# First stage of a hybrid decoder step: three engines in a written-out order, roots of row tiles in pairs, transposes woven into the first projections

## The chip, the cores and the metric

The kernel runs on one core of a Trainium2 chip. The metric is the device time of one execution in microseconds (us). Engines: PE (TensorE, matmuls; its weight loads are shown as PEld), DVE (VectorE), ACT (ScalarE), POOL (GpSimd), and SP, which issues the DMA loads and stores.

## The reference, cut to what matters

A gated-DeltaNet layer and an attention layer run over 1024 prompt rows and 8 sample rows of width 1024. The change lies in the first stage, which norms the rows and makes the first projections:

```python
def rmsnorm(x, g):
    xf = x.astype(jnp.float32)
    y = xf * lax.rsqrt(jnp.mean(xf * xf, axis=-1, keepdims=True) + EPS)
    return (y * g.astype(jnp.float32)).astype(x.dtype)

def gdn_layer(x, conv_buf, s0, norm_g, w_in, conv_w, a_log, dt_bias, o_norm, w_out):
    proj = rmsnorm(x, norm_g) @ w_in
    qkv, gate, a, beta_logit = jnp.split(proj, [...], axis=-1)
    qkv, new_buf = causal_conv_silu(qkv, conv_buf, conv_w)
    ...
```

## The kernel before

The 1032 rows lie in nine tiles `xt` of 128 rows (the ninth has 8). For each tile ACT squares the row and sums it (`junk`, `r`), DVE turns the sum into a reciprocal root (`rsqrt`: nine small operations on one column, each reading the one before), DVE scales the tile in place by root and gain (`xt`), PE transposes it in two halves of four 128x128 blocks into a PSUM buffer (`xps`, from a pool `gen` of two buffers), ACT copies each half out as its high part and DVE subtracts to get the low part (both into `xg`, which keeps every value as a sum of two). A half's buffer is free again when DVE's subtraction has read it.

Tiles 0 to 2 make group 0 of the columns (384), tiles 3 to 5 group 1 (384), tiles 6 to 8 group 2 (264). For each group PE then makes `psab` (16 matmuls with the small weight `wabp`, for the decay and beta logits) and two conv projections of head 0, key and query (24 matmuls each: high weight by high part, low weight by high part, high weight by low part). Each weight of 128 columns is loaded in two halves of 256 KB into `raw` (two buffers), copied by ACT (`whi`) and subtracted by DVE (`wlo`). Behind the projections come the gate projection of head 0 (weight `wz`), and, on a high priority, the chain from `abT` over `pst` and `ab` to `gf`, `psg` and `eG`: the decays. `cps` are the transposes of the conv taps and of the conv state, 24 small ones, into `cvT`. From the program's line 543 on (631 in the change) a planner written in the kernel has set the order by its own costs.

In the stage itself the tile framework's scheduler sets each engine's order from program order, priorities and its own estimates; the code says only what depends on what. SP issues the loads in the order of the string `LO` (digits are x tiles, `g` the gain, `k` and `q` the two weights), and eight DMAs may be under way at once; a ninth waits for an earlier one.

Of the kernel before, what the change touches and what calls it, by code (L numbers as in the profile page):

```python
# [57 lines left out]
def hybrid_step(  # L58
# [37 lines left out]
    def gps(name, dt=F32):  # L96
        return gen.tile([P, 512], dt, tag="gen", name=name)
# [8 lines left out]
    ident = cst.tile([P, P], F32, name="ident")  # L106
# [3 lines left out]
    ones = cst.tile([P, P], F32, name="ones")  # L110
# [75 lines left out]
    def load_w(col, src):  # L186
        hi = whl.tile([P, KT, P], F32R, tag="whi", name="whi")
        lo = whl.tile([P, KT, P], F32R, tag="wlo", name="wlo")
        load_split(hi, lo, src[:, col:col + P].rearrange("(k p) c -> p k c", p=P))
        return hi, lo  # L190

    def proj_group(hi, lo, xt_, gn, ps):
        i = 0
        for w_, part in ((hi, 0), (lo, 0), (hi, 1)):
            for k in range(KT):
                mm(ps[:, :gn], w_[:, k, :], xt_[:, part, k, :gn], i == 0, i == 3 * KT - 1)
                i += 1
                yield 0
# [33 lines left out]
    with tc.tile_pool(name="p2a", reuse_waits="tile", bufs=1) as p2a, \  # L232
# [39 lines left out]
        V.tensor_copy(wabp[:, :, 0:16], wab)
        V.tensor_tensor(out=wabp[:, :, 32:48], in0=wab, in1=wabp[:, :, 0:16].bitcast(F32), op=ALU.subtract)
        cvr = p2a.tile([28, 3072], F32, name="cvr")
        DMA.dma_start(out=cvr[0:24], in_=state_conv[0].rearrange("b i c -> (b i) c"))
        DMA.dma_start(out=cvr[24:28], in_=conv_w_a[0])
        sel = p2a.tile([64, 16], F32, name="sel")
        V.tensor_tensor(out=sel, in0=ident[:64, 0:16], in1=ident[:64, 32:48], op=ALU.add)
        abT = p2a.tile([64, T], F32, name="abT")

        def first_proj(gi):
# [5 lines left out]
            for j, w in enumerate(ws0):  # L287
                m = (1 - j) * H
                if gi == 0:
                    ues.append((0, m, 1 - j, conv_open(m)))  # L290
                ps = pj.tile([P, 512], F32, tag="pj", name="pj")
                for _ in proj_group(*w, xg[gi], gn, ps):
                    pass
                conv_evac(ues[j][3], m, gi, ps)

        for t in range(NT + 1):
            n = P if t < NT else NS
            g, off = divmod(t * P, 384)
            xt = xts[t]
            junk = p1.tile([P, D], BF16, tag="junk", name="junk", bufs=1)  # L300
            r = sm.tile([P, 1], F32, tag="r1", name="r1")
            S.activation(junk[:n], xt[:n], AF.Square, accum_out=r[:n])
            ri = sm.tile([P, 1], F32, tag="ss", name="ri")
            rsqrt(ri[:n], r[:n], 1, 1.0 / D, EPS, n, tag="b")
            V.scalar_tensor_tensor(out=xt[:n], in0=xt[:n], scalar=ri[:n], in1=gbc[:n], op0=ALU.mult, op1=ALU.mult)
            for hf in range(2):
                ps = gps("xps").rearrange("p (k t) -> p k t", k=4)
                for k in range(4):
                    PE.transpose(ps[:, k, :n], xt[:n, ts(4 * hf + k, P)], ident[:n, :n])
                hi = xg[g][:, 0, 4 * hf:4 * hf + 4, off:off + n]  # L310
                S.copy(hi, ps[:, :, :n])
                V.tensor_tensor(out=xg[g][:, 1, 4 * hf:4 * hf + 4, off:off + n], in0=ps[:, :, :n],
                                in1=hi.bitcast(F32), op=ALU.subtract)
            if t == CT:
                for q in range(2):
                    ps = gps("cps")
                    for j in range(12):
                        PE.transpose(ps[:, j * 28:j * 28 + 28], cvr[:, ts(12 * q + j, P)], ident[:28, :28])
                    S.copy(cvT[:, 12 * q:12 * q + 12, :].rearrange("p a b -> p (a b)"), ps[:, :12 * 28])
                V.tensor_scalar_mul(cvT[:, :, 24:28], cvT[:, :, 24:28], 0.5)  # L320
# [1546 lines left out]
```

## Time and profile before

| | |
|---|---|
| median of 3 runs | 1298.4 us (1294.66 to 1300.23) |
| profiled execution, its own time | 1299.52 us |
| its span, first to last instruction | 1297.8 us |
| mean granted TensorE clock | 0.985 |
| first `psab` matmul | 27.05 us |
| first matmul of the next stage (line 543) | 82.46 us |

The profile is that of one execution, with the start and the duration of each instruction. Consecutive instructions of one kind are merged in its timeline ("x8"). The duration of a merged row reaches from the start of the first to the end of the last. Matmuls are pipelined, so the end of one lies behind the start of the next.

### The profile page before, as it was taken

How to read it: one execution, taken by the hardware profiler on the slowest of the kernel's cores; microseconds unless marked ns; L12 is line 12 of the kernel's file. 1: busy time of each engine (PE TensorE's matmuls, PEld its weight loads, DVE VectorE, ACT ScalarE, POOL GpSimd, SP SyncE). 2: the span in 40 equal slices, each digit the busy share in tenths (PEclk: the TensorE clock that was granted, in tenths of full speed). 3: DMA queues.
4: the chain of work that ended last, by engine and by line, in shares of the span. 5: the costliest groups of instructions: out<-in, count | busy, mean ns of one | idle time of the engine just before them, and what ended most of it. 6: DMA issues, size and time to landing. Idle time of an engine off the chain costs nothing.

```text
span 1297.8 us, 24347 instructions
## 1 busy us (share of the span) xinstructions
PE 1223.9 (94%) x8887; PEld 1110.2 (86%) x8887; DVE 925.4 (71%) x2656; ACT 633.7 (49%) x1812; POOL 287.4 (22%) x404
## 2 busy tenths in 40 slices
PE   3999999999999999998999978999999999999998
PEld 3989898989999988888988756888889888888898
DVE  7468988878979897787976349587685677677221
ACT  5236555645455453545443127375574566666100
POOL 1036433424324353343301122111030020000000
PEclk9999999999999999998999979999999999999899
DMA  7021111110221322110256656111020021002322
GB/s 240 1 81 35 36 29 40 37 51 18 68 66 36 98 65 86 36 36 17 67 158 209 203 200 203 39 52 31 3 74 9 3 74 35 26 2 88 123 86 73
DMA packets 131988, 92.03 MB, mean 71 GB/s; under 512 B 33881, under 2 KB 123713, under 8 KB 131809
## 3 DMA queue, kind: packets, MB, share of 16 engines
q1 hardware_dynamic: 131868, 90.48, 23.6%
q8 instruction: 70, 1.15, 0.4%
q14 instruction: 50, 0.40, 0.1%
HBM read 69.28 MB, written 23.25 MB: 71 GB/s over the span
## 4 chain that ended last, share of the span: by engine, by line
PE 66%; DVE 20%; ACT 5%; DMA 4%; issue 3%; POOL 2%; SPq 1%; DVEq 0%; ACTq 0%; POOLq 0%
PE pj L543 24%; PE pj L100 15%; PE ivt L543 4%; DVE co L543 3%; PE chB L543 3%; PE sps L100 2%; PE chA L543 2%; PE op L100 2%; DMA out_dram<-hx 1%; PE ptp L1646 1%; DVE wqkv L82 1%; PE sp L543 1%; PE tq L1593 1%; DVE f L543 1%; PE psab L100 1%
## 5 line engine op out<-in xcount | busy, mean ns | idle before, releaser
L543 PE MATMUL pj<-xg,whi 128*128 128x384 f32 (+1 forms) x1392 | 289.3, 335 | 1.0 <-ACT whi L543 1.0
L543 PEld LDWEIGHTS pj<-xg,whi 128*128 128x128 f32 x1392 | 222.0, 190 | 2.7 <-ACT whi L543 1.2
L100 PE MATMUL pj<-wqkv,ng 128*128 128x384 f32 x768 | 154.2, 344 | 0.0
L543 PE MATMUL pj<-xg,wlo 128*128 128x384 f32 (+1 forms) x696 | 153.2, 337 | 0.0
L543 DVE SCALAR_TENSOR_TENSOR co<-ue,cvT,co 128x528 f32<-128x528 f32 x144 | 134.5, 940 | 16.1 <-ACT co L543 14.5
L100 PEld LDWEIGHTS pj<-wqkv,ng 128*128 128x128 f32 x768 | 132.3, 190 | 4.6 <-issue 4.2
L543 PEld LDWEIGHTS pj<-xg,wlo 128*128 128x128 f32 x696 | 112.9, 191 | 1.4 <-issue 0.7
L93 POOL TENSOR_TENSOR raw<-raw,gains 128x512 f32<-128x512 f32 x40 | 45.7, 1152 | 254.4 <-DMA raw<-in_w_in_b_dram 178.7
L100 PE MATMUL pj<-wob,oh 128*128 128x384 f32 (+1 forms) x576 | 97.9, 324 | 0.3 <-DVE hx L1828 0.3
L100 PEld LDWEIGHTS pj<-wob,oh 128*128 128x128 f32 x576 | 90.2, 190 | 1.1 <-DVE hx L1828 0.5
L543 PE MATMUL pj<-woa,ohl 128*128 128x512 f32 x288 | 76.1, 406 | 0.0
L543 PEld LDWEIGHTS pj<-woa,ohl 128*128 128x128 f32 x288 | 51.8, 188 | 11.5 <-issue 1.5
L1828 DVE TENSOR_TENSOR hx<-hx,pj 128x384 f32<-128x384 f32 (+3 forms) x27 | 13.7, 507 | 64.8 <-PE pj L100 35.8
L543 ACT COPY ue<-pj 128x384 f32<-128x384 f32 (+1 forms) x88 | 31.7, 377 | 52.8 <-PE pj L543 45.8
L543 POOL TENSOR_TENSOR ue<-ue,co 128x528 f32<-128x528 f32 x24 | 33.9, 1412 | 72.4 <-ACT ue L543 72.4
L543 DVE TENSOR_TENSOR wlo<-raw,whi 128x512 fp32r<-128x512 f32 x58 | 43.6, 757 | 7.6 <-ACT whi L543 7.4
L543 ACT ACTIVATE ue<-co 128x528 f32<-128x528 f32 x48 | 30.8, 644 | 30.2 <-DVE co L543 27.9
L543 ACT CAST whi<-raw 128x512 fp32r<-128x512 f32 x58 | 35.8, 619 | 16.9 <-PE pj L543 16.5
L100 PE MATMUL pj<-woa,ohl 128*128 128x512 f32 x96 | 28.7, 453 | 11.2 <-DVE ohl L1421 5.7
L543 POOL TENSOR_TENSOR co<-co,ue 128x528 f32<-128x528 f32 x24 | 39.0, 1623 | 1.3
L100 PE MATMUL sps<-kTh,qst 128*128 128x256 f32 (+1 forms) x144 | 37.5, 297 | 0.9 <-DVE m L1623 0.9
L100 PE MATMUL sps<-kTl,qst 128*128 128x256 f32 (+1 forms) x144 | 35.9, 297 | 0.5 <-DVE kTl L1600 0.5
(906 smaller groups left out, 2935.2 us busy)
## 6 DMA issues: line engine op xcount, KB each, us to landing
raw<-in_w_in_a_dram SPq DMA_DIRECT2D x64, 256.0 KB
ssm<-in_state_ssm_dram SPq DMA_DIRECT2D x32, 256.0 KB
hD<-hx SPq DMA_DIRECT2D x16, 512.0 KB
raw<-in_w_in_b_dram SPq DMA_DIRECT2D x32, 256.0 KB
xt<-in_x_prompt_dram SPq DMA_DIRECT2D x8, 512.0 KB
out_dram<-ssm SPq DMA_DIRECT2D x16, 256.0 KB
raw<-in_w_out_a_dram SPq DMA_DIRECT2D x16, 256.0 KB
hx<-in_x_prompt_dram SPq DMA_DIRECT2D x8, 512.0 KB
```

Source lines behind the costliest of these rows:

```text
L82: V.tensor_tensor(out=lo, in0=raw, in1=hi.bitcast(F32), op=ALU.subtract)
L93: G.tensor_tensor(out=raw, in0=raw, in1=gain[:, k:k + n].unsqueeze(2).broadcast_to([P, n, c]), op=ALU.mult)
L100: PE.matmul(out, lhsT, rhs, start=start, stop=stop, skip_group_check=True)
L543: op.f(*op.a, **op.k)
L1593: PE.transpose(tq[:, ts(h, P)], qhl[:, h].rearrange("p a d -> p (a d)"), identr)
L1646: PE.transpose(pp[:, ts(h, P)], pr[h // 2][:, h % 2, ts(kt, P)], ident)
L1828: V.tensor_tensor(out=hx[:n, :cn], in0=hx[:n, :cn], in1=ps[:n, :cn], op=ALU.add)
```

## The change

The order of PE, DVE and ACT in the stage is now that of the code (`manual_schedule`), in a sequence written by hand. Only tiles 0 to 2 are transposed ahead of the first `psab`. The other tiles' transposes stand between the first conv matmuls, half a tile after every four (`weave`). The roots are taken for tile 0, then in pairs (1 and 2, 3 and 4, 5 and 6, 7 and 8): the nine operations work on two columns. Squares of the next pair stand ahead of the copies of the pair before. The first weight (key) has a raw tile of its own, `wk_raw`, loaded by one DMA; the second (query) is loaded and split inside the weave. Loads go in the order `0g12a34k5678q`: `wab` ahead of tile 3, the key weight behind tile 4, the query weight last. The conv taps are turned in group 1's first conv projection and the copies of the conv state into `ue` (`conv_open`) come after the stage's projections.

```diff
-LO = "0g12k345q678"
-CT = 5
+LO = "0g12a34k5678q"
...
+        wk_raw = p1.tile([P, KT, P], F32, name="wk_raw")
+        wk = [whl.tile([P, KT, P], F32R, tag=f"w{a}", name=f"w{a}") for a in ("hi", "lo")]
+        ws0 = [wk]
...
+            elif o == "k":
+                DMA.dma_start(out=wk_raw, in_=w_in_a[0][:, H * P:H * P + P].rearrange("(k p) c -> p k c", p=P))
...
+        def turn(t):
...
+                S.copy(hi, ps[:, :, :n])
+                V.tensor_tensor(out=xg[g][:, 1, 4 * hf:4 * hf + 4, off:off + n], in0=ps[:, :, :n],
+                                in1=hi.bitcast(F32), op=ALU.subtract)
+                yield
...
+        def root(tiles):
+
+            n_ = len(tiles)
+            r, ri = (sm.tile([P, 2], F32, tag=g_, name="r1") for g_ in ("r1", "ss"))
+            for i, t in enumerate(tiles):
+                rts[t] = (r[:, i:i + 1], ri[:, i:i + 1])
+
+            def chain():
+                rsqrt(ri[:, :n_], r[:, :n_], n_, 1.0 / D, EPS, tag="b")
...
+        def weave(a_, b_, n):
+
+            for i, _ in enumerate(a_):
+                if i % n == n - 1:
+                    next(b_, None)
+            for _ in b_:
+                pass
...
+        with tc.manual_schedule(engines={mybir.EngineType.PE, mybir.EngineType.DVE, mybir.EngineType.Activation}):
+            chain = root([0])
+            sums(0)
+            chain()
+            scales(0)
+            chain = root([1, 2])
+            sums(1, 2)
+            for _ in turns([0]):
+                pass
+            chain()
+            scales(1, 2)
+            V.tensor_copy(wabp[:, :, 0:16], wab)
+            V.tensor_tensor(out=wabp[:, :, 32:48], in0=wab, in1=wabp[:, :, 0:16].bitcast(F32), op=ALU.subtract)
+            chain34 = root([3, 4])
+            sums(3, 4)
+            for _ in turns([1, 2]):
+                pass
+            chain34()
+            scales(3)
+            for a in range(2):
+                split(wk[0][:, ts(a, 4)], wk[1][:, ts(a, 4)], wk_raw[:, ts(a, 4)])
+            scales(4)
+            chain56 = root([5, 6])
+            sums(5)
+            first_ab(0)
+            sums(6)
+            chain78 = root([7, 8])
+            weave(first_conv(0, 0), seq(turns([3]), do(chain56), do(scales, 5), turns([4]), do(scales, 6), do(second_w), do(sums, 7, 8), turns([5])), 4)
...
+            weave(first_conv(0, 1), seq(turns([6]), do(chain78), do(scales, 7), do(scales, 8), turns([7, 8])), 4)
+            first_ab(1)
+            weave(first_conv(1, 0), turn_taps(), 10)
...
+        for j in range(2):
+            conv_open(ues[j][3], ues[j][1])
```

DVE before, where the roots of tiles 5, 6 and 7 lie around the scale and the subtractions of tile 5 (`xt_184`; `rs_x`, `rs_u` and `ri` are the small tiles of a root, with one line of `rsq_x` for each operation, L122 to L134):

```order
L132 TENSOR_TENSOR rs_u<-rs_u,ri 128x1
L128 SCALAR_TENSOR_TENSOR rs_u<-rs_x,ri 128x1
L122 TENSOR_SCALAR rs_x<-r_454 128x1
L133 SCALAR_TENSOR_TENSOR rs_u<-rs_u 128x1
L129 TENSOR_TENSOR rs_u<-rs_u,ri 128x1
L126 TENSOR_SCALAR ri<-rs_x 128x1
L134 SCALAR_TENSOR_TENSOR ri<-rs_u,ri 128x1
L130 SCALAR_TENSOR_TENSOR ri<-rs_u,ri 128x1
L128 SCALAR_TENSOR_TENSOR rs_u<-rs_x,ri 128x1
L305 SCALAR_TENSOR_TENSOR xt_184<-xt_184,ri,gbc 128x1024
L312 TENSOR_TENSOR xg_98<-xps,xg_98 128x4x128 x2
```

Operations of three tiles' roots take turns. In the change, on DVE from the subtractions of tile 6 (`xg_99`) on, the root of tiles 7 and 8 (`r_322`, `r_323`) and the scale of tile 7 (`xt_188`):

```order
L296 TENSOR_TENSOR xg_99<-xps,xg_99 128x4x128 x2
L121 TENSOR_SCALAR rs_x<-r_322 128x2
L125 TENSOR_SCALAR r_323<-rs_x 128x2
L127 SCALAR_TENSOR_TENSOR rs_u<-rs_x,r_323 128x2
L128 TENSOR_TENSOR rs_u<-rs_u,r_323 128x2
L129 SCALAR_TENSOR_TENSOR r_323<-rs_u,r_323 128x2
L130 TENSOR_TENSOR rs_u<-rs_x,r_323 128x2
L131 TENSOR_TENSOR rs_u<-rs_u,r_323 128x2
L132 SCALAR_TENSOR_TENSOR rs_u<-rs_u 128x2
L133 SCALAR_TENSOR_TENSOR r_323<-rs_u,r_323 128x2
L285 SCALAR_TENSOR_TENSOR xt_188<-xt_188,r_323,gbc 128x1024
```

One root stands by itself, behind the subtractions of tile 6 and ahead of the scale of tile 7. PE in the same place, before (`xt_184` is tile 5, `xt_196` tile 6, `xt_198` tile 7; `pj` are the conv matmuls of group 0):

```order
L100 MATMUL pj<-xg_97,whi 128x384 x9
L318 MATMUL cps<-ident,cvr 128x28 x24
L100 MATMUL pj<-xg_97,whi 128x384
L309 MATMUL xps<-ident,xt_196 128x128 x8
L100 MATMUL pj<-xg_97,whi 128x384 x6
L100 MATMUL pj<-xg_97,wlo 128x384 x6
L309 MATMUL xps<-ident,xt_198 128x128 x4
```

and in the change (`xt_184` tile 5, `xt_186` tile 6, `xt_188` tile 7):

```order
L293 MATMUL xps<-ident,xt_184 128x128 x4
L99 MATMUL pj<-xg_97,whi 128x384 x4
L293 MATMUL xps<-ident,xt_186 128x128 x4
L99 MATMUL pj<-xg_97,whi 128x384 x4
L293 MATMUL xps<-ident,xt_186 128x128 x4
L99 MATMUL pj<-xg_97,wlo 128x384 x4
L293 MATMUL xps<-ident,xt_188 128x128 x4
L99 MATMUL pj<-xg_97,wlo 128x384 x4
```

Every half tile has four conv matmuls behind it, and `cps` is gone from here. PE at the start of the gate projection (`pj` from `xg_97` on), before:

```order
L100 MATMUL pj<-xg_99,whi 128x264 x8
L100 MATMUL pj<-xg_97,whi 128x384 x8
L100 MATMUL pj<-xg_97,wlo 128x384 x2
L100 MATMUL psg<-gf,mle 128x64
L100 MATMUL psg<-gf,mgt 128x64
L100 MATMUL psg<-gf,ones 128x64
L100 MATMUL pss<-esd,ones 128x128
L100 MATMUL pj<-xg_97,wlo 128x384 x6
```

and in the change:

```order
L99 MATMUL pj<-xg_99,whi 128x264 x8
L99 MATMUL psg<-gf,mle 128x64
L99 MATMUL psg<-gf,mgt 128x64
L99 MATMUL psg<-gf,ones 128x64
L99 MATMUL pss<-esd,ones 128x128
L99 MATMUL pj<-xg_97,whi 128x384 x8
L99 MATMUL pj<-xg_97,wlo 128x384 x8
```

`psg` and `pss` have moved from inside the gate projection to ahead of it; on ACT the copies of the gate's weight have moved from ahead of `eG` to behind it, and on DVE its two subtractions from inside the chain from `ab` to `gf` to behind it.

## Rows read from the trace of the kernel before

**Rows 1.** The page: span, busy time of PE, and the chain that ended last, by engine.

```profile
span 1297.8 us, 24347 instructions
...
PE 1223.9 (94%) x8887; PEld 1110.2 (86%) x8887; DVE 925.4 (71%) x2656; ACT 633.7 (49%) x1812; POOL 287.4 (22%) x404
...
PE 66%; DVE 20%; ACT 5%; DMA 4%; issue 3%; POOL 2%; SPq 1%; DVEq 0%; ACTq 0%; POOLq 0%
```

**Rows 2.** Windows: us, busy time of each engine, granted PE clock, DMA share, GB/s.

```profile
0.00:27.00 27.00, 7.43 (x32) 6.29 (x33) 19.19 (x83) 16.84 (x31) 4.44 (x19) 1.00 0.85 262
27.00:83.00 56.00, 54.90 (x359) 52.45 (x358) 26.53 (x93) 16.79 (x38) 0.77 (x4) 1.00 0.12 42
553.00:556.40 3.40, 3.40 (x17) 3.40 (x16) 2.63 (x4) 0.87 (x2) 3.00 (x3) 0.50 0.03 5
```

**Rows 3.** Timeline of PE: start, us, what, x count [idle before].

```profile
11.29 1.94 PE L309 MATMUL xps<-ident,xt 128*128 128x128 f32 x8 [11.29 <-DVE xt L305]
17.03 1.97 PE L309 MATMUL xps<-ident,xt 128*128 128x128 f32 x8 [3.79 <-DVE xg L312]
21.23 1.97 PE L309 MATMUL xps<-ident,xt 128*128 128x128 f32 x8 [2.24 <-DVE xg L312]
...
27.05 4.03 PE L100 MATMUL psab<-xg,wabp 128*128 128x384 f32 x12
...
34.09 0.60 PE L309 MATMUL xps<-ident,xt 128*128 128x128 f32 x4
...
37.88 1.67 PE L318 MATMUL cps<-ident,cvr 28*128 28x28 f32 x24
...
46.55 0.84 PE L100 MATMUL pst<-sel,abT 64*128 64x16 f32 x6
47.32 3.08 PE L100 MATMUL psab<-xg,wabp 128*128 128x384 f32 x16
...
70.38 0.41 PE L100 MATMUL psg<-gf,mle 128*128 128x64 f32 x2
...
82.46 1.68 PE L543 MATMUL pj<-xg,whi 128*128 128x384 f32 x8 [0.99 <-ACT whi L543]
```

**Rows 4.** Timeline of DVE, first stage.

```profile
8.12 0.15 DVE L122 TENSOR_SCALAR rs_x<-r 128x1 f32<-128x1 f32 x1 [2.63 <-ACT junk L302]
...
9.86 1.28 DVE L305 SCALAR_TENSOR_TENSOR xt<-xt,ri,gbc 128x1024 f32<-128x1024 f32 x1
...
26.84 1.28 DVE L305 SCALAR_TENSOR_TENSOR xt<-xt,ri,gbc 128x1024 f32<-128x1024 f32 x1
28.03 1.28 DVE L312 TENSOR_TENSOR xg<-xps,xg 128x512 fp32r<-128x512 f32 x2
29.23 0.15 DVE L132 TENSOR_TENSOR rs_u<-rs_u,ri 128x1 f32<-128x1 f32 x1
29.29 0.16 DVE L128 SCALAR_TENSOR_TENSOR rs_u<-rs_x,ri 128x1 f32<-128x1 f32 x1
...
63.02 0.29 DVE L335 COPY ab<-pst 128x128 f32<-128x128 f32 x1 [4.47 <-PE pst L100]
...
67.87 0.68 DVE L82 TENSOR_TENSOR wlo<-raw,whi 128x512 fp32r<-128x512 f32 x1
...
70.01 0.22 DVE L369 COPY gf<-z 128x64 f32<-128x64 f32 x1
```

**Rows 5.** Timeline of the SP queue.

```profile
16.71 0.97 SPq L257 DMA_DIRECT2D xt<-in_x_prompt_dram  x2
```

**Rows 6.** Timeline of ACT, first stage.

```profile
6.94 1.06 ACT L302 ACTIVATE junk<-xt 128x1024 bf16<-128x1024 f32 x1 [2.88 <-DMA xt<-in_x_prompt_dram]
...
20.57 1.13 ACT L81 CAST whi<-raw 128x512 fp32r<-128x512 f32 x2
...
71.28 0.33 ACT L381 ACTIVATE eG<-psg 128x192 f32<-128x192 f32 x1 [1.05 <-PE psg L100]
```

**Rows 7.** Timeline of PE at 552 us.

```profile
552.30 0.66 PE L543 MATMUL otp<-ident,osb 128*128 128x128 f32 x4 [2.08 <-DVE m L543]
```

More of the change, by code (lines that the diff above doesn't have):

```diff
@@ L258, in load_x @@
             xts.append(xt)
-        ws0 = []
+        wab = p2a.tile([P, KT, 16], F32, name="wab")
+        wk_raw = p1.tile([P, KT, P], F32, name="wk_raw")
+        wk = [whl.tile([P, KT, P], F32R, tag=f"w{a}", name=f"w{a}") for a in ("hi", "lo")]
+        ws0 = [wk]
+        wabp = p2a.tile([P, KT, P], F32R, name="wabp")
+        V.tensor_scalar_mul(wabp, ones.unsqueeze(1).broadcast_to([P, KT, P]), 0.0)
+        sel = p2a.tile([64, 16], F32, name="sel")
+        V.tensor_tensor(out=sel, in0=ident[:64, 0:16], in1=ident[:64, 32:48], op=ALU.add)
         for o in LO:
@@ L272, in hybrid_step @@
[L272 to L273 removed]
+            elif o == "a":
+                DMA.dma_start(out=wab, in_=w_in_a[0, :, 4096:4112].rearrange("(k p) c -> p k c", p=P))
+            elif o == "k":
+                DMA.dma_start(out=wk_raw, in_=w_in_a[0][:, H * P:H * P + P].rearrange("(k p) c -> p k c", p=P))
+            elif o != "q":
+                load_x(int(o))
         cvr = p2a.tile([28, 3072], F32, name="cvr")
[L275 removed]
@@ L276, in hybrid_step, with square, scale @@
-        DMA.dma_start(out=cvr[24:28], in_=conv_w_a[0])
-        sel = p2a.tile([64, 16], F32, name="sel")
-        V.tensor_tensor(out=sel, in0=ident[:64, 0:16], in1=ident[:64, 32:48], op=ALU.add)
         abT = p2a.tile([64, T], F32, name="abT")
-        def first_proj(gi):
+        def square(t, r):
+            n = P if t < NT else NS
+            junk = p1.tile([P, D], BF16, tag="junk", name="junk", bufs=1)
+            S.activation(junk[:n], xts[t][:n], AF.Square, accum_out=r[:n])
+        def scale(t, ri):
+            n = P if t < NT else NS
+            xt = xts[t]
+            V.scalar_tensor_tensor(out=xt[:n], in0=xt[:n], scalar=ri[:n], in1=gbc[:n], op0=ALU.mult, op1=ALU.mult)
@@ new lines, in turn @@
+        def turn(t):
+            n = P if t < NT else NS
+            g, off = divmod(t * P, 384)
+            for hf in range(2):
+                ps = gps("xps").rearrange("p (k t) -> p k t", k=4)
+                for k in range(4):
+                    PE.transpose(ps[:, k, :n], xts[t][:n, ts(4 * hf + k, P)], ident[:n, :n])
+                hi = xg[g][:, 0, 4 * hf:4 * hf + 4, off:off + n]
+                S.copy(hi, ps[:, :, :n])
+                V.tensor_tensor(out=xg[g][:, 1, 4 * hf:4 * hf + 4, off:off + n], in0=ps[:, :, :n],
+                                in1=hi.bitcast(F32), op=ALU.subtract)
+                yield
@@ new lines, in hybrid_step, with sums @@
+        rts = {}
+        def root(tiles):
[5 more added lines that the diff above has]
+                rsqrt(ri[:, :n_], r[:, :n_], n_, 1.0 / D, EPS, tag="b")
+            if NT in tiles:
+                V.memset(r, 1.0)
+            return chain
+        def sums(*tiles):
+            for t in tiles:
+                square(t, rts[t][0])
@@ L282, in first_proj, with scales, turns, first_ab @@
+        def scales(*tiles):
+            for t in tiles:
+                scale(t, rts[t][1])
+        def turns(tiles):
+            for t in tiles:
+                yield from turn(t)
+        def first_ab(gi):
             g0, gn = GRP[gi]
@@ L286, in first_proj @@
             S.copy(abT[:, g0:g0 + gn], ps[:64, :gn])
[L287 to L320, printed above, removed]
@@ L321, in hybrid_step, with first_conv @@
-        for gi in range(3):
-            first_proj(gi)
+        def first_conv(gi, j):
+            if gi == 0:
+                ues.append((0, (1 - j) * H, 1 - j, uep.tile([P, 1060], F32, tag="ue", name="ue")))
+            ps = pj.tile([P, 512], F32, tag="pj", name="pj")
+            yield from proj_group(*ws0[j], xg[gi], GRP[gi][1], ps)
+            conv_evac(ues[j][3], (1 - j) * H, gi, ps)
+        def weave(a_, b_, n):
[4 more added lines that the diff above has]
+                pass
@@ new lines, in turn_taps, with second_w @@
+        def turn_taps():
+            for q in range(2):
+                ps = gps("cps")
+                for j in range(12):
+                    PE.transpose(ps[:, j * 28:j * 28 + 28], cvr[:, ts(12 * q + j, P)], ident[:28, :28])
+                S.copy(cvT[:, 12 * q:12 * q + 12, :].rearrange("p a b -> p (a b)"), ps[:, :12 * 28])
+                yield
+            V.tensor_scalar_mul(cvT[:, :, 24:28], cvT[:, :, 24:28], 0.5)
+        def second_w():
+            ws0.append(load_w(0, w_in_a[0]))
@@ new lines, in do, with seq @@
+        def do(f, *a):
+            f(*a)
+            yield from ()
+        def seq(*gs):
+            for g_ in gs:
+                yield from g_
+        with tc.manual_schedule(engines={mybir.EngineType.PE, mybir.EngineType.DVE, mybir.EngineType.Activation}):
[26 more added lines that the diff above has]
+            weave(first_conv(0, 0), seq(turns([3]), do(chain56), do(scales, 5), turns([4]), do(scales, 6), do(second_w), do(sums, 7, 8), turns([5])), 4)
+            DMA.dma_start(out=cvr[0:24], in_=state_conv[0].rearrange("b i c -> (b i) c"))
+            DMA.dma_start(out=cvr[24:28], in_=conv_w_a[0])
+            weave(first_conv(0, 1), seq(turns([6]), do(chain78), do(scales, 7), do(scales, 8), turns([7, 8])), 4)
+            first_ab(1)
+            weave(first_conv(1, 0), turn_taps(), 10)
@@ L323, in hybrid_step @@
+        for _ in first_conv(1, 1):
+            pass
+        first_ab(2)
+        for j in range(2):
+            for _ in first_conv(2, j):
+                pass
+        for j in range(2):
+            conv_open(ues[j][3], ues[j][1])
         hd[0]["og"] = ogs[:, 0]
```

11 lines of the change are left out of this document (1 added, 10 removed).

## The prediction

> **What bounds the kernel now.** The page first: TensorE (PE) is busy 94% of the span, and the chain of work that ended last is 66% PE, 20% VectorE (DVE) [rows 1]. So an edit is worth what it does to PE's idle time and to the speed at which PE runs. The windows come next, since the change touches one stage. In the first 27 us PE works 7.43 us; in the next 56 us it works 54.90 [rows 2]. DVE is the reverse: 19.19 of the first 27, 26.53 of the next 56. So the stage has two halves. Until the first `psab` matmul at 27.05 PE waits (11.29, 3.79 and 2.24 us ahead of the transposes of tiles 0, 1 and 2 [rows 3]), for an `xt` that DVE has scaled or for a PSUM buffer that DVE has read. From there PE is the bound, and the transposes of tiles 4 to 8, the conv taps and the first `pst` lie inside a full PE stream that reaches the next stage (L543) at 82.46 [rows 3]. The reader should keep these two points, 27.05 and 82.46. Behind 82.46 both versions issue the same rows in the same order on every engine (in SP's queue one cache copy, out of any path, has moved ahead of two weight loads), so what the change does to 82.46 it does to the end, unless a wait behind it absorbs the shift.
>
> **DVE's prices.** A root chain is nine small operations. Alone, each waits for the one before: from 8.12 to the scale at 9.86 is 1.74 us, 0.193 each [rows 4]. Interleaved with another tile's chain they start 0.06 apart (29.23, 29.29) [rows 4]. So the kernel before pays about 0.6 us for most of its nine chains. A 128x2 chain is not in the trace; a 128x1 operation takes what little it does for its fixed part, so I take 1.74 for a pair (below it could only be the interleaved 0.6; above, nothing in the rows suggests more than double, 3.5). A scale occupies 1.19 (26.84 to 28.03), a pair of subtractions (`xg`, or the two halves of `wlo`) 1.20 (28.03 to 29.23) [rows 4].
>
> The pairing is the place where a rule speaks for the change. The Trainium skill, page "VectorE: DVE Perf Modes", section "The DRAIN you can't avoid", says that the next operation does not start until the pipe has emptied, so one should minimise the number of operations. By it nine chains of nine would cost 81 x 0.193 = 15.6 us and five 8.7, a saving of 6.9. The starts 0.06 apart disagree: operations of 0.15 overlap when they do not depend on each other.
>
> With the rows, the old chains cost about 1.74 + 1.9 + 7 x 0.6 = 7.8 us of DVE (an estimate), the five new ones, which nothing is interleaved with, 5 x 1.74 = 8.7. The pairing gains nothing; fixing the order takes the interleaving away.
>
> **The change, walked through.** I put the new rows one after another on the three engines with these prices.
>
> *To psab.* Tile 0 is unchanged until its scale ends at 11.15. Its subtractions now go ahead of the next chain (13.1 to 14.5), the chain of tiles 1 and 2 ends at 16.2, their scales at 18.6. Tile 1 is transposed from 17.65, tile 2 from 20.1, and `psab` starts at 21.8, 5.2 us before 27.05, because only three tiles are turned ahead of it and no weight is split there. Loads are no limit: the kernel before issues tiles 6 and 7 at 16.71, behind weights that wait for a buffer [rows 5]; now all x loads stand ahead of any such wait, behind only `wab` and one load of 512 KB for the first weight. At the mean 262 GB/s of the first 27 us [rows 2] the 4.2 MB up to tile 5 take 16 us and are there before 20; its square comes at 23.6. Tile 7 and the second weight (another 1.6 MB, 6 us) are there before 26, and used from 31.7.
>
> *The weave.* Here PE needs, tile by tile, what DVE makes. DVE finishes the subtractions of tile 2 at 23.3. Until the scale of tile 7 it has, in order: three chains (5.2), five scales (6.0), four halves of `wlo` (2.4) and the subtractions of tiles 3 to 6 (4.8), 18.4 us, plus some 1.4 waiting for ScalarE (ACT) copies that stand behind squares of 1.06 and weight copies of 1.13 [rows 6]: 43.2. PE has from 21.8 until tile 7 only 16 `psab`, 36 conv matmuls and the 32 transposes of tiles 3 to 6: 52 x 0.18 + 32 x 0.11 = 12.9 us, and 1.1 more for a `psab` that starts slow (0.18: sixteen in 3.08, the last one's tail of 0.2 taken off; 0.11: four in 0.60, less the same tail [rows 3]). So it must wait for the rest of the 21.6 us up to 43.4: by the walk 0.3 and 0.7 for tiles 3 and 4, 1.8 for tile 5, 1.3 for tile 6 and 3.9 for tile 7, 8.0 in all (the 0.6 over the difference of the sums are tails). From there 3.7 us remain (12 conv matmuls, the last three half tiles), and `psab` of group 1 starts at 47.1. Before, it starts at 47.32 [rows 3]. The head start of 5.2 us has gone into the weave: **-0.2**.
>
> *What is owed.* At 47.32 the kernel before has already turned the taps (1.67 us) and done its first three `pst` (0.84) [rows 3]. The new order does them in group 1: **+2.5** (less some 0.1 of tails, taken as 2.4).
>
> *psg.* Before, `psg` at 70.38 comes when ten gate matmuls already run, so DVE's chain from `ab` at 63.02 to `gf` at 70.01 is hidden [rows 3, 4]. Now PE must issue `psg` before the gate. Without the two `wlo` in it (67.87 and one more; some 0.95 us) that chain takes 6.0 to 6.45 us after `pst`, while PE has 44 matmuls of 264 columns, some 5.45 (0.18 x 264/384 each): **+1.0**, less the 0.1 of before. The gate's weight copies now stand on ACT behind `eG`, which started 0.90 after `psg` (71.28) [rows 3, 6]; 0.3 of `eG` and 0.6 of a copy later the gate may start, 1.8 after `psg`, while `psg` and `pss` fill 1.27, minus semaphores: **+0.7**. Bounds: 0, if DVE is 1.6 faster there, and 2.5.
>
> Sum so far: -0.2 + 2.4 + 0.9 + 0.7 = **+3.8**.
>
> **The clock.** Until about 31 us PE's matmuls run at half speed: 12 of 384 columns take 4.03, later 16 take 3.08 [rows 3], which is 1.2 against 2.4 GHz. I let half of the new `psab` run slow; all or none changes the sum by +2.8 or -0.5. Then, after the stall of 2.08 at 550.2, the windows show a granted clock of 0.50 from 553.0 to 556.4 [rows 2, 7]. The weave has stalls of 1.8 and 3.9, so one such stretch is likelier than none: PE would do half of its work in 3.4 us from 43.4, **+1.6** (0 without it; 2.8 if it is twice as long).
>
> The Trainium skill, page "TensorE: Matmul & The Clock Gate", Part 1, says the same in general: throttled is the default, activity releases it and idleness brings it back. The trace agrees at 553. The rule doesn't say which of the weave's stalls count, so the term keeps its bounds.
>
> Total +5.4: 1299.5 of the profiled execution becomes 1304.9. That execution is 1.1 over the median of the runs, so I forecast 1298.4 + 5.4 = **1303.8 us**, +0.42%, within 0.5% (6.5 us), which is about what a measurement of this kernel can tell from no change.
>
> **Rivals.**
> 1. *Slower: the clock stays low through the weave.* With waits in it from 31.7 to 43.4, PE may run at half speed from about 36 to 50, and the whole of `psab` too: 3.7 + 2.8 in place of 1.6 gives 3.8 + 6.5 = +10.3, 1308.7. For it: in the first 27 us, with stalls of 2 to 4 us between bursts, the speed did not rise. Against: there PE worked 7.43 of 27 us, in the weave it works more than half of the time. It decides from a second low stretch on.
> 2. *Faster: DVE is paid by the count of operations, or overlaps more than I allow.* If the 6.9 us saved by the count were real, tile 7 would be ready that much sooner, and the stalls of 8.0 us in the weave would nearly go: 3.8 - 6.9 = -3.1, 1295.3. With every stall of the weave and of `psg` gone it is -5.9, 1292.5, still not 0.5%. For it: `psab` does start early. Against: the starts 0.06 apart.
> 3. *It moves nothing at the end.* The next stage could absorb the shift if its first waits had an earlier cause. Against: PE's wait of 0.99 at 82.46 is for weight copies [rows 3] that stand behind the last gate operation on ACT in both orders, so they shift too. Time 1298.4.
>
> **How the numbers follow.** Forecast (3.8 to 6.5) 0.50, rival 1 0.20, rival 2 0.16, rival 3 0.14. Slower by over 0.5% is rival 1 and a fifth of the forecast, 0.30; faster by over 0.5% is the far end of rival 2, 0.05; within 0.65. The range 1295 to 1308 leaves out half of rival 1 and the ends of rival 2 and is at most 2 in 10; the forecast's own is 1301 to 1306.
>
> **What would show it.** In the new trace: `psab` near 21.8; DVE's nine 128x2 operations 0.19 apart with nothing between them; PE idle for 3 to 4 us ahead of tile 7's transposes for DVE's scale; `psab` of group 1 near 47; an idle PE ahead of `psg` and of the first gate matmul; L543's first matmul (L631 now) at 86 to 88. I am wrong if PE has no stall over 1 us in the weave, or if L631 starts before 82 us, or if the end doesn't shift as the stage does.

## The result, and the profile after

The changed kernel takes 1307.24 us (median of 20 runs, 1298.16 to 1314.03) against 1297.9 us (20 runs, 1293.39 to 1301.0) for the kernel before: ratio 1.0071, 95% interval 1.0056 to 1.0086, or 9.3 us more. The wide range of the prediction, 1295 to 1308, held it near its upper end; the forecast's own, 1301 to 1306, did not. The forecast was too small by about 4 us, and the likelier class, within 0.5%, did not come; slower by over 0.5% did.

The page of the changed kernel, to be read against [rows 1]:

```profile
span 1305.9 us, 24307 instructions
...
PE 1226.9 (94%) x8887; PEld 1112.1 (85%) x8887; DVE 928.0 (71%) x2621; ACT 633.8 (49%) x1812; POOL 286.6 (22%) x404
```

The span is 8.1 us longer than in [rows 1], PE is busy 3.0 us longer for the same 8887 matmuls. Both are small against the whole, so the stage itself must be read. The timeline of PE there (start, duration, what, count, idle before and its releaser):

```profile
21.99 4.71 PE L99 MATMUL psab<-xg,wabp 128*128 128x384 f32 x16
...
33.97 0.66 PE L293 MATMUL xps<-ident,xt 128*128 128x128 f32 x4 [1.90 <-DVE xg L296]
...
37.56 0.66 PE L293 MATMUL xps<-ident,xt 128*128 128x128 f32 x4 [1.08 <-DVE xg L296]
...
39.12 0.96 PE L99 MATMUL pj<-xg,wlo 128*128 128x384 f32 x4
43.82 1.09 PE L293 MATMUL xps<-ident,xt 128*128 128x128 f32 x4 [3.75 <-DVE xt L285]
44.56 1.63 PE L99 MATMUL pj<-xg,wlo 128*128 128x384 f32 x4
...
50.34 3.09 PE L99 MATMUL psab<-xg,wabp 128*128 128x384 f32 x16
...
75.14 0.41 PE L99 MATMUL psg<-gf,mle 128*128 128x64 f32 x2 [0.91 <-DVE gf L457]
...
76.92 2.93 PE L99 MATMUL pj<-xg,whi 128*128 128x384 f32 x8 [0.51 <-ACT whi L80]
...
91.06 1.68 PE L631 MATMUL pj<-xg,whi 128*128 128x384 f32 x8 [0.98 <-ACT whi L631]
```

`psab` of group 0 starts 5.06 us sooner than in [rows 3], `psab` of group 1 3.02 us later, the next stage 8.60 us later (82.46 to 91.06); the end moves by 8.1. So the whole loss lies in the stage. Behind the wait of 3.75 us, four conv matmuls take 1.63 us instead of 0.96. The windows cut at that point (us, busy time of PE, its weight loads, DVE, ACT and POOL with counts, granted PE clock, DMA share, GB/s):

```profile
37.56:42.70 5.14, 2.51 (x16) 2.15 (x16) 3.61 (x13) 1.17 (x2) 0.00 (x0) 1.00 0.87 302
42.70:49.50 6.80, 5.68 (x22) 5.15 (x23) 3.74 (x5) 1.36 (x3) 0.00 (x0) 0.50 0.00 0
49.50:76.80 27.30, 26.00 (x185) 24.40 (x184) 8.83 (x43) 7.13 (x20) 0.57 (x3) 1.00 0.00 1
76.80:80.20 3.40, 3.28 (x10) 3.28 (x11) 1.33 (x3) 0.59 (x2) 0.00 (x0) 0.50 0.39 104
```

Two stretches lie at the lower level (1.2 GHz, granted clock 0.50): 6.80 us around tile 7, behind the waits of 1.90, 1.08 and 3.75, and 3.40 us behind the waits of 0.91 and 0.51. In between the clock is full. (These views also read 1.00 for the first 25 us, as [rows 2] does for its first 27; there the spacing of the matmuls tells more: up to 25.65 us those of `psab` start 0.32 us apart, half speed, and 0.18 apart behind that.) What makes tile 7 late is DVE, in its timeline:

```profile
40.62 0.16 DVE L121 TENSOR_SCALAR rs_x<-r 128x2 f32<-128x2 f32 x1
40.82 0.17 DVE L125 TENSOR_SCALAR r<-rs_x 128x2 int32<-128x2 int32 x1
...
42.20 0.16 DVE L133 SCALAR_TENSOR_TENSOR r<-rs_u,r 128x2 f32<-128x2 f32 x1
42.39 2.47 DVE L285 SCALAR_TENSOR_TENSOR xt<-xt,r,gbc 128x1024 f32<-128x1024 f32 x2
```

The nine operations of a 128x2 root start 0.2 us apart, one block of 1.77 us (40.62 to 42.39) with nothing between them, and the scale of tile 7 stands behind it.

### The profile page after: what moved, and what is told of

It reads as the page before. It is cut to its first block, busy times and chain, and to the rows that moved or that the text cites. A ratio compares the mean times of both kernels' runs of the same rounds, so it can differ in the third digit from the quotient of the medians.

```text
span 1305.9 us, 24307 instructions
## 1 busy us (share of the span) xinstructions
PE 1226.9 (94%) x8887; PEld 1112.1 (85%) x8887; DVE 928.0 (71%) x2621; ACT 633.8 (49%) x1812; POOL 286.6 (22%) x404
## 4 chain that ended last, share of the span: by engine, by line
PE 64%; DVE 21%; ACT 5%; DMA 4%; issue 3%; POOL 2%; SPq 1%; DVEq 0%; ACTq 0%; POOLq 0%
PE pj L631 23%; PE pj L99 14%; PE ivt L631 4%; DVE co L631 3%; PE chB L631 3%; PE sps L99 2%; PE chA L631 2%; PE op L99 2%; DMA out_dram<-hx 1%; PE ptp L1734 1%; DVE wqkv L81 1%; DVE f L631 1%; PE xps L293 1%; PE tq L1681 1%; PE psab L99 1%
```

## The experiments

Theory A: the written order makes DVE late, since whole root chains stand in the way of the next tile, and makes PE wait for `psg` and the gate; the waits then take the clock down. Its rivals: the waits cost and the clock doesn't; the pairs, the weave or the loads cost, and not the fixing of the order. All twelve kernels were timed in five rounds against the kernel before. "Next stage" is the start of its first matmul in the profiled execution. That is one execution, and it can lie well off its kernel's median: e6's took 1296.66 us (median 1302.15), e12's 1297.44 (median 1292.45).

| kernel | next stage, us (before 82.46) | ratio to before, 95% interval |
|---|---|---|
| changed kernel | 91.06 | 1.0071 (1.0056 to 1.0086) |
| e1, wait ahead of tile 7 filled | 86.47 | 1.0045 (1.0018 to 1.0073) |
| e2, taps ahead of tile 7 | 87.39 | 1.0041 (1.0017 to 1.0065) |
| e3, gate's weight early | 86.95 | 1.0046 (1.0023 to 1.0068) |
| e4, one root for tiles 5 to 8 | 93.41 | 1.0092 (1.0065 to 1.0120) |
| e5, kernel before with pairs alone | 82.56 | 1.0003 (0.9989 to 1.0016) |
| e8, changed kernel, order left to the scheduler | 79.00 | 0.9975 (0.9962 to 0.9988) |
| e12, e8 with single roots | 77.96 | 0.9972 (0.9958 to 0.9987) |
| e9, DVE's order alone left to it | 84.23 | 1.0017 (1.0003 to 1.0032) |
| e10, PE's order alone left to it | 87.62 | 1.0041 (1.0022 to 1.0060) |
| e6, written order, roots spread | 82.42 | 1.0019 (1.0001 to 1.0038) |
| e7, e6 with weight subtractions on GpSimd | 84.99 | 1.0029 (1.0009 to 1.0049) |
| e11, e8 with taps in the weave | 78.11 | 0.9962 (0.9940 to 0.9984) |

The two columns go together: taken as 1298 us times the ratio, each kernel's time lies within some 2.5 us of 1298 plus its shift of the next stage. What is done in the stage is what is paid at the end. The intervals of e1 to e4 and of e10 overlap with the changed kernel's, so what each of these edits is worth is read from one trace each, and the times only agree with it; those of e6 to e9, e11 and e12 do not overlap with it.

### The clock, and the single waits

**e1.** 20 matmuls into a PSUM tile that nobody reads, ahead of tile 7's transposes; they only add work.

```diff
-do(scales, 8), turns([7, 8])), 4)
+do(scales, 8), do(fill, 20), turns([7, 8])), 4)
```

> The changed kernel with 20 matmuls of 384 columns more, whose result nobody reads, on PE in the idle 3.75 us ahead of tile 7's transposes. If the granted clock is what costs (theory A: the stall of 3.75 us lets the clock fall to 0.50 from 42.7 to 49.5), the fill keeps PE busy, the clock stays at 1.00 there, the matmuls behind tile 7 run at 0.18 us each and not 0.36, psab of group 1 starts at 47 to 48 in place of 50.34, L631's first matmul near 88 in place of 91.06, and the time is about 3 us below the changed kernel's. If only the stall itself counts (rival), nothing moves: psab at 50 to 51, L631 at 91 to 92, time as the changed kernel's or 0 to 1 us above.

PE of e1:

```profile
21.89 3.09 PE L99 MATMUL psab<-xg,wabp 128*128 128x384 f32 x16
...
39.35 3.68 PE L99 MATMUL dum<-xg,wabp 128*128 128x384 f32 x20
43.27 0.63 PE L293 MATMUL xps<-ident,xt 128*128 128x128 f32 x4 [0.24 <-DVE xt L285]
...
47.26 3.09 PE L99 MATMUL psab<-xg,wabp 128*128 128x384 f32 x16
...
72.05 0.41 PE L99 MATMUL psg<-gf,mle 128*128 128x64 f32 x2 [0.90 <-DVE gf L462]
...
73.83 1.68 PE L99 MATMUL pj<-xg,whi 128*128 128x384 f32 x8 [0.51 <-ACT whi L80]
...
86.47 1.68 PE L636 MATMUL pj<-xg,whi 128*128 128x384 f32 x8 [0.98 <-ACT whi L636]
```

and its window over the same stretch as above:

```profile
42.70:49.50 6.80, 6.56 (x43) 5.70 (x43) 3.33 (x6) 1.92 (x5) 0.00 (x0) 1.00 0.00 0
```

Work that is good for nothing brings `psab` of group 1 forward by 3.08 us. Filling the wait cannot shorten it: tile 7 still comes at 43.27, 0.55 us sooner than in the changed kernel, with the first `psab` at full speed here (3.09 us, not 4.71). The other 2.53 us are the clock's: from tile 7's transposes to `psab` it is 3.99 us instead of 6.52. The other 1.5 us of the 4.6 at the next stage come from the gate, which this time starts at full speed (1.68 for eight, not 2.93) behind the same two waits of 0.90 and 0.51. So these waits alone do not bring the clock down, and that the fill, and no such chance, kept it up at tile 7 rests on this one execution.

**e2.** `turn_taps()` moved between `do(scales, 8)` and `turns([7, 8])`.

> The changed kernel with the turn of the conv taps moved from group 1's projection into the second weave, between the scale of tile 8 and tile 7's transposes, so that it fills PE's stall there. Theory A: the stall of 3.75 us ahead of tile 7 splits or shrinks to at most 2 us, the clock does not fall (or half as long), the 2.4 us owed for taps and pst are gone but for the 0.8 of pst: psab of group 1 at 46 to 47.5, L631 at 85 to 86.5, time 4.5 to 6 us below the changed kernel's. Rival (stall and clock as before, only the taps hidden): psab at 50.3, L631 at 89 to 89.5, time 1.6 to 2 us below. Rival (taps cost nothing where they stood, since PE waits later anyway): L631 at 91.

PE of e2:

```profile
43.49 0.63 PE L293 MATMUL xps<-ident,xt 128*128 128x128 f32 x4 [0.29 <-DVE xt L285]
...
46.66 0.41 PE L293 MATMUL xps<-ident,xt 8*128 8x8 f32 x4 [0.73 <-DVE xg L296]
...
48.15 4.32 PE L99 MATMUL psab<-xg,wabp 128*128 128x384 f32 x15
```

and a window of it:

```profile
49.20:52.60 3.40, 3.40 (x13) 3.40 (x12) 0.00 (x0) 0.10 (x1) 0.00 (x0) 0.50 0.00 0
```

The wait is gone, `psab` stands at 47.00 and the taps are no longer owed, as theory A said. But the clock falls all the same, now at 49.20 and for 3.4 us, behind 24 taps' transposes of 28 columns and waits of 0.29, 0.26 and 0.73; and it falls again at the gate, from 73.07 to 76.48, as in the changed kernel. The next stage at 87.39 lies between the two expectations.

**e3.** The gate's weight in one load into the first weight's raw tile, between the two weaves.

```diff
+            wz_raw = p1.tile([P, KT, P], F32, tag="wr", name="wz_raw")
+            DMA.dma_start(out=wz_raw, in_=w_in_a[0][:, 3 * H * P:3 * H * P + P]...)
...
-        wz = load_w(3 * H * P, w_in_a[0])
+        for a in range(2):
+            split(wz[0][:, ts(a, 4)], wz[1][:, ts(a, 4)], wz_raw[:, ts(a, 4)])
```

> The changed kernel with the gate's weight loaded between the two weaves by one DMA into the raw tile of the first weight and split from there, so that PE's first ten gate matmuls stand ahead of psg again, ACT's copies ahead of eG and the two subtractions in the chain from ab to gf. Theory A: the waits of 0.91 ahead of psg and 0.51 ahead of the gate and the half clock from 76.8 to 80.2 go: L631 at 87.5 to 88.5 in place of 91.06, time 2.5 to 3.5 us below the changed kernel's. Rival (the fall of the clock at 76.8 comes from elsewhere, e.g. as a late effect of the weave): the stalls go, the low stretch stays, L631 at 89.5 to 90, time 1 to 1.5 below.

PE of e3:

```profile
49.09 3.09 PE L99 MATMUL psab<-xg,wabp 128*128 128x384 f32 x16
...
74.84 0.41 PE L99 MATMUL psg<-gf,mle 128*128 128x64 f32 x2
...
86.95 1.68 PE L635 MATMUL pj<-xg,whi 128*128 128x384 f32 x8 [0.99 <-ACT whi L635]
```

`psg` and the gate wait for nothing. From `psab` of group 1 to the next stage it is 37.86 us against 40.72: 2.86 less, within what theory A expected: 1.4 us of waits, and about as much of the low stretch behind them. The remaining 1.25 of the 4.11 come mostly from a shorter low stretch in the weave (43.9 to 47.3, 3.4 us instead of 6.8), which this edit had not aimed at.

**e4.** One root for tiles 5 to 8, 128x4.

```diff
-            chain56 = root([5, 6])
-            sums(5)
+            chain56 = root([5, 6, 7, 8])
+            sums(5, 6, 7, 8)
```

> The changed kernel with one root for tiles 5 to 8 in place of two pairs (their four squares stand ahead of group 0's copies on ACT), which takes one chain of nine dependent operations (1.77 us) off DVE ahead of tile 7's scale. Theory A: tile 7's transposes start 1.5 to 2 us sooner, at about 45.5 to 46 in place of 47.6 (the wait ahead of them about 2 in place of 3.75), and the clock's fall is shorter or gone: psab of group 1 at 46 to 48.5, L631 at 86.5 to 89.5, time 1.5 to 4.5 us below the changed kernel's. Rival (ACT's squares of tiles 7 and 8 are the new limit, since they now stand ahead of tile 3's copies by 2.1 us): tile 5's and 6's transposes later by 1 to 2 us, L631 at 90.5 to 92, no gain.

ACT, DVE and PE of e4:

```profile
28.65 1.06 ACT L280 ACTIVATE junk<-xt 128x1024 bf16<-128x1024 f32 x1 [5.26 <-issue]
```

```profile
27.28 1.28 DVE L285 SCALAR_TENSOR_TENSOR xt<-xt,r,gbc 128x1024 f32<-128x1024 f32 x1
28.51 0.06 DVE L313 MEMSET r<- 128x4 f32 x1
```

```profile
34.95 1.12 PE L293 MATMUL xps<-ident,xt 128*128 128x128 f32 x4 [6.17 <-DVE xg L296]
...
47.21 0.63 PE L293 MATMUL xps<-ident,xt 128*128 128x128 f32 x4 [1.98 <-DVE xt L285]
```

Neither expectation held. (Its 47.6 for tile 7 in the changed kernel is a slip: the trace has 43.82.) The wait ahead of tile 7 shrinks to 1.98, as theory A said, but a worse one appears: ACT idles 5.26 us ahead of the first square, and PE 6.17 us ahead of tile 4. The profile names no releaser; the square writes into the root's tile, and the memset of that tile stands in DVE's written order behind the scale of tile 4, 0.14 us ahead of the square. So, by order and times, one operation of 0.06 us in the wrong place holds up three engines; no run moved the memset, so this is argued and not shown.

### The order

**e5.** The kernel before, its order the scheduler's, with the roots in pairs and nothing else.

> The kernel before (scheduler's order, its loads, its split of the weights) with one part of the change alone: the roots of tiles 1 to 8 in pairs. Theory A (the old chains were interleaved, and PE is the bound from 27 us on): the chains are again interleaved with wide operations, psab of group 0 starts within 1 us of 27.05, the next stage's first matmul comes at 81.5 to 83.5 (82.46 before), time within 0.2% of before. Rival (DVE is paid by the count of operations, 36 fewer at 0.193): psab starts 3 to 5 us sooner, the next stage's first matmul at 78 to 80, time 2.5 to 4.5 us below before.

`psab` starts at 27.29 (27.05 before), the next stage at 82.56, ratio 1.0003. The pairs by themselves are worth nothing, as theory A expected.

**e8.** The changed kernel with the fixed sequence taken off.

```diff
-        with tc.manual_schedule(engines={mybir.EngineType.PE, mybir.EngineType.DVE, mybir.EngineType.Activation}):
+        if True:
```

> The changed kernel without the fixed sequence: the same code, pairs, loads and weave order as program order, but the scheduler sets the order of PE, DVE and ACT. Its DVE order has the roots' operations between wide ones again, and on PE ten gate matmuls stand ahead of psg. Theory A (the written order is what makes tile 7 late and PE wait for psg and the gate): no wait over 2 us from psab on, no low clock from 42 to 50 and from 76 to 80, the taps still owed: the next stage's first matmul at 84 to 86.5 (91.06 in the changed kernel, 82.46 before), time 4 to 7 us below the changed kernel's and 1 to 4 above before. Rival (pairs, weave and loads cost the time, not the fixing of the order): 89 to 91, time within 2 us of the changed kernel's.

DVE of e8:

```profile
18.16 0.16 DVE L121 TENSOR_SCALAR rs_x<-r 128x2 f32<-128x2 f32 x1
18.23 0.68 DVE L81 TENSOR_TENSOR wlo<-wk_raw,whi 128x512 fp32r<-128x512 f32 x1
...
36.89 2.46 DVE L285 SCALAR_TENSOR_TENSOR xt<-xt,r,gbc 128x1024 f32<-128x1024 f32 x2
```

PE and a window of it:

```profile
38.32 1.07 PE L293 MATMUL xps<-ident,xt 128*128 128x128 f32 x8
...
79.00 1.68 PE L631 MATMUL pj<-xg,whi 128*128 128x384 f32 x8 [0.98 <-ACT whi L631]
```

```profile
22.00:48.00 26.00, 26.00 (x169) 24.33 (x167) 18.04 (x38) 12.31 (x24) 0.34 (x2) 1.00 0.20 66
```

The same code in the scheduler's order is 12.06 us ahead of the changed kernel at the next stage and 3.46 us ahead of the kernel before; it beats both. PE is busy for 26.00 of 26.00 us. DVE puts the first weight's subtractions and single operations of a root into the time in which it would wait, and scales tile 7 at 36.89, 5.50 us sooner. Theory A's direction was right and its size (84 to 86.5) too small; the rival falls.

**e12.** e8 with one chain for each tile.

> The scheduler-ordered kernel (0.9975 of before) with the roots of tiles 1 to 8 one by one again instead of in pairs. Theory A (where operations of other tiles lie between them, 36 more small operations cost DVE some 0.06 each, 2.2 us, and PE has slack for it or not): next stage's first matmul at 79 to 81.5, time 0 to 2.5 us above the scheduler-ordered kernel's, still at or under before. Rival (the gain of the scheduler-ordered kernel is the pairing): next stage at 82 or later, time as before.

One row of PE of e12, and a window from its `psab` to the next stage:

```profile
47.87 1.51 PE L99 MATMUL pst<-sel,abT 64*128 64x16 f32 x12
```

```profile
22.00:78.00 56.00, 54.89 (x362) 52.15 (x361) 30.73 (x113) 20.56 (x47) 0.67 (x4) 1.00 0.18 60
```

36 more operations cost nothing that can be seen: ratio 0.9972 against 0.9975, next stage at 77.96 against 79.00 (e8 has a low stretch of 3.4 us, shown under e11, and e12 has none). So what e8 gains over the kernel before is in neither the pairs nor the fixed order. By exclusion it lies in the rest, the loads, the weave as program order, the raw tile and the new places of the taps and `conv_open`, which were not taken apart.

**e9 and e10.** `manual_schedule` for PE and ACT alone (DVE free), and for DVE and ACT alone (PE free).

> The changed kernel with PE's and ACT's order written out as before, but DVE's order left to the scheduler (and, as a consequence of its model, ten gate matmuls ahead of psg again). Theory D (it is DVE's written order, with whole chains as blocks, that makes tile 7 late): tile 7's transposes at 39 to 41 in place of 43.8, the wait ahead of them under 1.5 us, the next stage's first matmul at 79 to 83 (91.06 in the changed kernel, 79.00 with all three engines free), time 6 to 10 us below the changed kernel's. Theory E (DVE can only fill what ACT's fixed copies and squares hand it, so ACT's order counts as much): tile 7 at 42 to 44, a wait of 2 to 4 us stays, next stage at 85 to 88, time 3 to 5 us below the changed kernel's, most of it from the gate.

> The changed kernel with DVE's and ACT's order written out as before, but PE's order left to the scheduler, which moves the 16 psab matmuls of group 1 ahead of tile 7's transposes; psg stays ahead of the gate. Theory D (DVE makes tile 7 late, whatever PE does): tile 7 at 43 to 44 as before, but PE has 2.9 us of psab to do in the wait, so the wait there is under 1.5 us and the low clock from 42.7 goes; the waits of 1.4 us at psg and gate stay: next stage's first matmul at 85.5 to 88, time 3 to 5 us below the changed kernel's. Rival (the fixed PE order is the whole of the loss): 79 to 82, time 8 to 12 below.

PE of e9, of e10, and a window of e10:

```profile
40.83 0.63 PE L293 MATMUL xps<-ident,xt 128*128 128x128 f32 x4 [2.28 <-DVE xt L285]
```

```profile
43.97 1.06 PE L293 MATMUL xps<-ident,xt 128*128 128x128 f32 x8 [0.41 <-DVE xt L285]
...
46.96 1.88 PE L354 MATMUL cps<-ident,cvr 28*128 28x28 f32 x16
...
74.98 1.68 PE L99 MATMUL pj<-xg,whi 128*128 128x384 f32 x8 [0.51 <-ACT whi L80]
```

```profile
46.80:57.00 10.20, 10.20 (x48) 9.67 (x47) 0.25 (x2) 1.37 (x4) 0.34 (x2) 0.50 0.00 0
```

Freeing DVE gives back 6.83 us of the 12.06, freeing PE 3.44. Neither is the whole, and neither figure is that order's alone. In e9 ten gate matmuls stand ahead of `psg` again, and its two waits are gone; 5.52 of the 6.83 are there at `psab` of group 1 (44.82 against 50.34). In e10 the gate ran at full speed behind the same two waits (0.92 and 0.51), which is worth 1.5 us of the 3.44 and came in e1 without any change of order. In e9 tile 7 comes 3 us sooner but still behind a wait of 2.28, between theories D and E; the fixed orders of ACT (the squares and weight copies that DVE needs) and PE are what it left in place; no run frees ACT alone. In e10 tile 7 is as late as ever, 43.97, as theory D said, and PE fills the time with `psab`; the wait shrinks to 0.41, yet the low stretch is not gone but longer, 10.20 us, behind small waits (0.41, 0.96, 0.19) and small matmuls.

### Towards a better kernel

**e6 and e7.** The written order kept, with one to four operations of a root after each scale or subtraction, the taps in the second weave and e3's early weight; e7 has the four `wlo` subtractions on GpSimd.

```diff
                 V.tensor_tensor(out=xg[g][:, 1, ...], in0=ps[:, :, :n], in1=hi.bitcast(F32), op=ALU.subtract)
+                steps(1)
                 yield
...
-            weave(first_conv(0, 1), seq(turns([6]), do(chain78), do(scales, 7), do(scales, 8), turns([7, 8])), 4)
+            rest()
+            scales(7)
+            weave(first_conv(0, 1), seq(turns([6]), do(scales, 8), turn_taps(), turns([7, 8])), 3)
```

> The changed kernel, still in a written order, with the roots of tiles 3 to 8 spread: one to four of the nine operations at a time between DVE's scales and subtractions instead of one block each; square 6 ahead of group 0's copy; tile 7's scale ahead of the subtractions of tile 6; the taps in the second weave ahead of tile 7; the gate's weight loaded early, so that ten gate matmuls stand ahead of psg. Theory A (DVE's dependent chains set the weave): tile 7's transposes at 39 to 41.5 in place of 43.8, no wait over 1.5 us in the weave, granted clock 1.00 from 26 us on, psab of group 1 at 42.5 to 45, the next stage's first matmul at 78.5 to 81, time 1.5 to 4 us below before. Rival (the chains are not the bound; DVE's wide operations and ACT's copies keep tile 7 late): tile 7 at 43 or later, next stage at 82.5 to 85, time as before or up to 2 us above.

> The spread kernel with the four subtractions for the low parts of the two conv weights on GpSimd, which has nothing to do there, in place of DVE. Theory A (DVE still sets the weave): tile 7 another 1 to 2.4 us sooner, the next stage's first matmul 1 to 2.4 us ahead of the spread kernel's. Rival (PE sets the weave once the chains are spread, or the subtractions of 1.13 us each come too late for the matmuls of the low weight): no gain, 0 to 1 us later.

DVE and PE of e6:

```profile
37.48 1.28 DVE L285 SCALAR_TENSOR_TENSOR xt<-xt,r,gbc 128x1024 f32<-128x1024 f32 x1
38.69 1.28 DVE L296 TENSOR_TENSOR xg<-xps,xg 128x512 fp32r<-128x512 f32 x2
```

```profile
39.42 0.93 PE L365 MATMUL cps<-ident,cvr 28*128 28x28 f32 x12 [1.89 <-DVE xg L296]
```

Spreading the roots brings the scale of tile 7 from 42.39 to 37.48, so theory A is right on DVE. The gain is not delivered: the scale now stands ahead of tile 6's subtractions, `cps` waits 1.89 us for the PSUM buffer that they free, and tile 7's transposes stand behind `cps`, at 42.67. The next stage comes at 82.42, next to the rival's 82.5 to 85, for another reason, and the ratio of 1.0019 puts e6 some 2.5 us above the kernel before. In e7 GpSimd takes four subtractions off DVE and nothing comes of it: 84.99, 2.57 later, with a low stretch of 6.8 us (41.4 to 48.2) where e6 has one of 3.4 (42.3 to 45.7). The theory of e7 falls; how much of the 2.57 is the clock's was not separated, and by their times the two kernels cannot be told apart (ratios 1.0019 and 1.0029).

**e11.** e8 with the taps in the second weave (`turn_taps()` ahead of `turns([7, 8])`, half a tile after every three).

> The scheduler-ordered kernel (0.9975 of before) with the taps and their copies moved in program order to the second weave, a half tile after every three conv matmuls. Theory (the low clock from 51 to 54.4 there follows on the 60 small matmuls of cps and pst between 44.4 and 49.7): with the 24 of cps away from pst that low stretch is gone, the next stage's first matmul comes at 76.5 to 78 in place of 79.00, time 1 to 2.5 us below the scheduler-ordered kernel's. Rival (no link with the small matmuls): next stage at 78.8 to 79.5, no change.

Windows of e8, and one of e11:

```profile
45.70:51.00 5.30, 5.30 (x42) 4.95 (x41) 0.21 (x1) 0.92 (x3) 0.34 (x2) 1.00 0.01 3
51.00:54.40 3.40, 3.40 (x12) 3.40 (x11) 1.54 (x2) 0.87 (x2) 0.00 (x0) 0.50 0.01 2
```

```profile
22.00:78.00 56.00, 54.99 (x364) 52.02 (x362) 29.12 (x85) 20.18 (x45) 1.77 (x3) 1.00 0.19 59
```

The low stretch of e8 is gone, and the next stage comes 0.89 us sooner, a little less than expected. That the small matmuls had brought the stretch on is not shown: e12 has the same `cps` and `pst` rows between 44.89 and 50.2 and no low stretch. e8, e11 and e12 cannot be told apart in time; all three are faster than both kernels.

## Why the prediction was right and where it failed

**The walk through the weave** held. `psab` at 21.99 (21.8 forecast), waits of 1.90, 1.08 and 3.75 ahead of tiles 5, 6 and 7 (1.8, 1.3, 3.9), tile 7 at 43.82 (43.4), a 128x2 root 1.77 (1.74). The small waits ahead of tiles 3 and 4 did not come. `psab` ran slow for eleven of its sixteen matmuls, not for half; in e1, where all ran fast, waits of 0.65 and 0.44 stand ahead of tiles 3 and 4, and tile 7 comes 0.55 us sooner. Two sums are off by little: 0.60 less a tail of 0.2 makes 0.10 for a transpose, not 0.11, and the waits of 8.0 are 0.4 over the difference of the sums, not 0.6. Neither moves tile 7, which hangs on DVE.

**What is owed** (+2.4) and **`psg` and gate** (+0.9, +0.7) were about right: 0.91 and 0.51 in the trace, and e3, which takes both waits and their low stretch away, gains 2.86. For the taps and `pst`: from `psab` of group 1 to `psg` it is 24.80 us, 23.89 without the wait, against 23.06 in [rows 3], which hold ten gate matmuls of 0.18 more, so about 2.6.

**The clock** (+1.6) is the term that was mis-sized. From tile 7's transposes to `psab` of group 1 there are 6.52 us; the prediction had 3.7, and e1, at full clock, has 3.99. So the clock's share is 2.5, not 1.6, near the upper bound of 2.8 that it had kept. A second low stretch at the gate, worth 1.5 us (e1's gate to next stage takes 12.64 us, the changed kernel's 14.14), had no term at all. These two, 0.9 and 1.5, are most of the 3.2 us by which the stage (+8.60) missed the forecast (+5.4), and they put the next stage at 91.06, outside the 86 to 88 that it had named; 0.4 of a later tile 7 and 0.3 in the rows behind it are the rest. None of its signs of being wrong came. Rival 1, the clock low through the weave, was to decide "from a second low stretch on". A second one came, but at the gate; its +10.3 is nearer to the measured +9.3 than the forecast's +5.4. That the wide range held the time is in part luck: it reached up to 1308 for half of this rival, and the time came there by other terms. The prediction looked at the weave's long waits and took the two short ones later for their own length only.

The Trainium skill, page "TensorE: Matmul & The Clock Gate", Part 1, has activity release the clock and idleness bring it back. e1 agrees: with PE kept busy the granted clock was 1.00 from 42.70 to 49.50. e8 does not: its clock was 0.50 from 51.00 on, though PE was busy for all of the 5.30 us before, in part with small matmuls. Nor did the rule let one foretell the second stretch: behind the same waits of 0.9 and 0.51 it came in the changed kernel and not in e1.

**The pairing** gains nothing, as forecast: e5 and e12. Rival 2, with its 6.9 us saved by the count of operations, is out. The Trainium skill, page "VectorE: DVE Perf Modes", section "The DRAIN you can't avoid", has an operation wait until the pipe is empty, but adds that a next operation which is not held back starts earlier. The prediction left out the second half, and the rows go by it: in e8 the `wlo` subtraction starts 0.07 us after the root operation of 0.16 ahead of it (18.16, 18.23).

**The cause behind the walk** was named but not priced. The prediction said that fixing the order takes the interleaving away, and then added up a DVE that is packed from 23.3 on. e8 shows that 5.50 us of tile 7's lateness were the order's: the first weight's subtractions and the next root fit into waits ahead of 22 us. e9 gives 2.99 of them to DVE's own order. Left to the scheduler, the same code is 12.06 us ahead at the next stage. **Rival 3** is out: the end moved by 8.1 of 8.6 us.

## What to carry over

A written order must be better than the one it replaces on every engine that it fixes: price the gaps that the scheduler was filling, single dependent operations first, and try the new code without the fixed order before keeping it. Where PE is the bound, a wait on it costs its length and can cost a stretch at half clock behind it (2.5 us behind tile 7's); in e1 filler work of no use came out cheaper than that stretch. After moving a step, look for what now queues behind it: a PSUM buffer freed 1.9 us late undid the gain of e6, and, as argued above, a memset of 0.06 us that of e4.

## What the hardware did that was not expected

The low stretches of PE's clock are not fixed by the program's rows alone. The waits of about 0.91 and 0.51 at `psg` and gate were followed by a clock of 0.50 in the changed kernel, e2 and e4, and by full clock in e1 and e10; the rows of `cps` and `pst` by a low stretch in e8 and none in e12. A low stretch of 3.4 us cost 1.5 us at the gate. The changed kernel's runs spread over 16 us (1298.16 to 1314.03) with mean granted clocks from 0.989 in the fastest to 0.978 in the slowest, and the runs of the kernel before beside them over 7.6.
